# Projections with tokens outermost, one pool for weight buffers, and layer-2 masks on VectorE, in a two-layer decoder trunk

## The chip, the cores and the metric

The kernel runs on one core of one Trainium2 chip. The metric is device time in microseconds (us) of one execution. Before the change the median of three runs is 376.45 us (376.45, 374.06 and 377.89).

## What is computed

Two layers, each on a sequence of 256 tokens of width 1024; batch 1, everything float32.

```python
for l in range(2):
    mod = c @ w_ada[l] + b_ada[l]                 # -> shift, scale, gate, 1024 each
    u   = x * (1 + scale) + shift
    h   = u @ w_in[l]                             # one projection, columns split among groups
    o   = concat[DSA(4 heads), FoX(6 heads), NSA(6 heads)] * silu(h_gate)
    x   = LayerNorm(4 ** 0.25 * x + (1 + gate) * (o @ w_out[l]))
# DSA: causal attention over 64 keys picked per token by an indexer (scores, top-k -> mask)
# FoX: causal attention with a cumulative forget term added to the scores
# NSA: two causal branches and one over compressed keys, mixed by gates
# masked softmax: s = where(mask, s, -inf); e = exp(s - max(s)); e / sum(e)
```

## The kernel before, in words

The 256 tokens are two blocks t0 and t1 of 128. Heads go in pairs; a layer makes 11 calls of `attn_pair`: 2 for DSA, 6 for NSA (3 pairs, 2 branches each) and 3 for FoX.

**Weights.** All of them come from one packed array as a stream of pieces of 128 x 1024 floats (512 KB), in a fixed order. SP issues the loads (L487, in `load_more`); a load waits for a free slot among 6 "raw" buffers. A piece of a projection weight is then split in two: ACT casts it to fp32r, the high part wh (L518, `split_hi`); DVE subtracts wh from raw, which gives the low part wl (L536, `split_lo`). The raw slot is free once wl is written. There are 5 wh and 5 wl buffers, free when the last matmul of the piece is done (`piece_done`). Each product of two such operands is three matmuls on PE (`mm3`, L551 to L553). Pieces of the conditioning weight w_ada aren't split: DVE multiplies and sums each in one instruction (L585, "ada").

**Order.** Each engine runs its instructions in one fixed order. A planner (`Order`) makes it when the program is built: every part of the work is a task with a priority, an engine and a modelled cost, and the task that could go and has the smallest priority number goes next. `PR` (L364) holds the priorities (`nsa1=5.08`: NSA of layer 2, and so on) and the orders of tiles (`tord0`, `tord1`).

**Stages.** Layer 1 takes 64 pieces for its chunks A to D (token-major products: q, k, v, gates) as they arrive. Then come 16 "tiles" T (L551 with 128x256 outputs; 8 hold FoX and NSA operands, 8 the output gate), interleaved with rope (L643 to L646), transposes of it (L657), attention, and the ada pieces of layer 2.

**Attention.** In `attn_pair` PE writes the scores of two heads for t0 (128 columns each) and t1 (256 columns) into PSUM (L724); FoX adds its cumulative term by a matmul (L729), and the mask is added by another: L732 adds the DSA mask, L734 the causal triangle. DVE takes the negated row maximum (L679), ACT the exponential from PSUM with the row sum (L683), DVE the reciprocal of the sums (L669 on), ACT the normalisation (L696); PE transposes (L706), ACT copies to SBUF (L710), PE multiplies with V (L755).

**Output projection.** Eight pieces O.n.q (n: half of the 1024 columns, q: quarter of the contraction). The loop is n outside t: n0 for t0 and t1 (512 columns each), then n1 for t0 and for t1, in two blocks of 256 columns each. After each block `resid` runs on DVE: times gate (L1229), plus scaled x (L1232), row statistics (L1234). When a token block has all of its columns, the mean and variance follow (L1244, L1245), a reciprocal square root on ACT and DVE (L1291 to L1295), and for layer 1 `next_u`: transposes of the normalised rows (L1376), their high part uH and low part uL (L1402) for layer 2. In layer 2 the rows are finished (t0: L1280, L1286; t1: L1301, L1304) and stored.

**Layer 2** begins with chunks in the order D, C, A, B (`proj_tok`): for D the loop is t outside q, so that t0 can begin before t1 is ready; for C, A and B it is q outside t.

Of the kernel before, what the change touches and what calls it, by code (L numbers as in the profile page):

```python
# [362 lines left out]
RW = [6, 5]  # L363
PR = dict(zn='VV', upart=4, ul='VVVV', nrm='AAAA', cord='DCAB', t1q=0, cuts=(0, 512, 1024), oq=(0, 1, 2, 3), tord=(0, 1, 2, 3, 4, 5, 6, 7, 8, 9, 10, 11, 12, 13, 14, 15), gpp=(0, 1), res=-3.5, warm=10, tol=0.1, ada_at=(10, 0.5), adag_at=((0, 0.5), (8, 1)), ow=(512, 256), aff=0.49, tw=512, nact=((0, 0), (1, 0), (0, 1), (1, 1)), pro='', gp0=(0, 1), gp1=(0, 1), acc=5, s=2, pt=1, o=3, ms=3, side=8, topk=3, idx=2, dec=0.5, cmp=1.2, nsa=1.6, dsa=1.7, fox=1.8, gate=4, gate1=6, ada=6, main=10, ev=0, split=4, nahead=2, acc1=1.5, cmp1=3, dec0=0.28, nsa1=5.08, topk1=5.9, nsa0=1.3, dec1=0.5, idx1=0.64, tord1=(2, 4, 6, 7, 0, 1, 8, 9, 5, 3, 14, 10, 12, 13, 11, 15), dsa0=0.12, oq0=(1, 0, 2, 3), cmp0=1.39, fox1=1.95, dsa1=4.17, fox0=1.48, oq1=(1, 3, 2, 0), topk0=3, tord0=(0, 1, 3, 4, 5, 6, 7, 8, 9, 10, 11, 12, 13, 2, 14, 15), idx0=2, nrm1='AAAA', nrm0='AAAA', t1q0=0, t1q1=0)  # L364
# [3 lines left out]
def trunk(ctx: ExitStack, tc: tile.TileContext, xT, x, crow, wst, bcol, lnrow, pe_b, cst, cstb, out,  # L368
# [105 lines left out]
    def load_more():  # L474
        while nload[0] < len(order):
# [10 lines left out]
            t = wp.tile([P, 1024], F32, tag="raw", name=nm("raw"), bufs=RAW)  # L486
# [39 lines left out]
    def split_lo(key, on_pool):  # L526
# [5 lines left out]
        lo = wp.tile([P, 1024], F32R, tag="wl", name=nm("wl"), bufs=WH)  # L532
        if on_pool:
            G.tensor_tensor(lo[:, :n], raw, h[:, :n].bitcast(F32), op=ALU.subtract)
        else:
            V.tensor_tensor(lo[:, :n], raw, h[:, :n].bitcast(F32), op=ALU.subtract)  # L536
# [3 lines left out]
        raw_done()  # L540
# [228 lines left out]
    def layer(l, uH, uL):  # L769
# [211 lines left out]
        def dsa_pair(i, prio):  # L981
# [499 lines left out]
```

## Time and profile before

| | |
|---|---|
| median of three runs | 376.45 us |
| the profiled execution | 374.79 us |
| its span (first to last instruction) | 373.0 us |
| mean granted TensorE clock in it, as a share of full speed | 0.978 |
| instructions | 6834 |
| weights moved on SP's queue | 74.75 MB |

The span is cut here in six stages: 0 to 58.4 us is the chunk projections of layer 1 with their loads; to 146.6 us tiles and attention up to the last DSA scores; to 172.8 us the rest of the attention and the last tiles; to 221.4 us the output projection of layer 1, the hand-over to layer 2 and its chunks D and C; to 363.1 us the rest of layer 2, to its last matmul; then the end. In the table of windows "PEclk" is the clock that TensorE was granted, "DMA share" the mean busy share of 16 DMA engines. In a list of instructions in order of time, square brackets hold the time for which the engine stood idle just before and what ended it.

### The profile page before, as it was taken

Reading aid. Unit: us, or ns where it says so; the run is one execution under the profiler, and the core shown is the slowest. Engines: PE = TensorE matmul, PEld = TensorE weight load, DVE = VectorE, ACT = ScalarE, POOL = GpSimd, SP = SyncE. Lnnn points to the kernel's source line nnn. Section 1 sums busy time; section 2 is a strip of 40 time slices with the busy share of each in tenths; the row PEclk is TensorE's granted clock in tenths of the full one; section 3 lists DMA queues with packets and bytes.
Section 4 is the critical chain, followed back from the end, with each engine's and each line's share of the span. In section 5 each row is a group of like instructions: output and inputs, shape, how many; then the busy total and the mean of one; then the engine's idle time right before and its main releaser. Section 6 shows DMA issues by size and latency. Waiting matters only on the chain.

```text
span 373.0 us, 6834 instructions
## 1 busy us (share of the span) xinstructions
PE 344.9 (92%) x2430; PEld 282.7 (76%) x2430; DVE 314.8 (84%) x771; ACT 251.7 (67%) x656; POOL 2.5 (1%) x10
## 2 busy tenths in 40 slices
PE   6899999699999997879987999999999999999990
PEld 2688769579887785777986888678887887887890
DVE  5798889999989989889979985989988894666876
ACT  3554566769898785595558764667897868997420
POOL 2000000000000000000000000000000000000000
PEclk9899999989999999899999999999999999999996
DMA  6999999456763167979728486543436865123003
GB/s 217 416 406 402 352 368 397 152 160 210 238 205 126 57 183 222 317 241 330 253 71 268 146 293 192 162 123 112 128 104 199 306 198 197 58 59 112 1 2 112
DMA packets 22074, 75.47 MB, mean 202 GB/s; under 512 B 2964, under 2 KB 3096, under 8 KB 21912
## 3 DMA queue, kind: packets, MB, share of 16 engines
q1 hardware_dynamic: 21752, 74.75, 59.5%
q8 instruction: 19, 0.31, 0.3%
q10 hardware_dynamic: 288, 0.29, 0.2%
q14 instruction: 15, 0.12, 0.1%
HBM read 73.98 MB, written 1.05 MB: 201 GB/s over the span
## 4 chain that ended last, share of the span: by engine, by line
PE 70%; DMA 12%; DVE 11%; ACT 4%; issue 2%; SPq 0%; DVEq 0%; ACTq 0%
PE b L551 16%; PE b L553 15%; PE b L552 15%; DMA raw<-in_wst_dram 12%; PE b L724 5%; PE b L755 5%; PE b L706 4%; DVE raw L585 2%; DVE wl L536 2%; ACT wh L518 2%; PE b L657 2%; PE b L734 2%; PE b L908 2%; ACT t2k L1384 1%; PE b L627 1%
## 5 line engine op out<-in xcount | busy, mean ns | idle before, releaser
L518 ACT CAST wh<-raw 128x1024 fp32r<-128x1024 f32 (+2 forms) x81 | 83.2, 1028 | 48.6 <-DMA raw<-in_wst_dram 29.8
L536 DVE TENSOR_TENSOR wl<-raw,wh 128x1024 fp32r<-128x1024 f32 (+2 forms) x81 | 96.0, 1193 | 14.4 <-ACT wh L518 13.4
L551 PE MATMUL b<-uH,wh 128*128 128x256 f32 x256 | 78.0, 305 | 0.0
L552 PE MATMUL b<-uL,wh 128*128 128x256 f32 x256 | 73.0, 285 | 0.0
L553 PE MATMUL b<-uH,wl 128*128 128x256 f32 x256 | 73.0, 285 | 0.0
L585 DVE SCALAR_TENSOR_TENSOR raw<-raw,cbc 128x1024 f32<-128x1024 f32 x48 | 58.2, 1217 | 3.9 <-DMA raw<-in_wst_dram 3.8
L553 PE MATMUL b<-wh,uL 128*128 128x512 f32 (+1 forms) x128 | 50.6, 395 | 2.7 <-DVE uL L1358 1.5
L551 PE MATMUL b<-wh,uH 128*128 128x512 f32 (+1 forms) x128 | 51.0, 399 | 2.0 <-ACT uH L1356 2.0
L551 PEld LDWEIGHTS b<-uH,wh 128*128 128x128 f32 x256 | 49.7, 194 | 2.0 <-issue 1.3
L552 PE MATMUL b<-wl,uH 128*128 128x512 f32 (+1 forms) x128 | 50.2, 392 | 0.3 <-DVE wl L536 0.3
L552 PEld LDWEIGHTS b<-uL,wh 128*128 128x128 f32 x256 | 49.8, 194 | 0.0
L553 PEld LDWEIGHTS b<-uH,wl 128*128 128x128 f32 x256 | 49.5, 193 | 0.1
L683 ACT ACTIVATE p<-b,nmx 128x128 f32<-128x128 f32 x88 | 36.3, 427 | 1.5 <-DVE nmx L679 1.4
L696 ACT ACTIVATE p<-p,rinv 128x128 f32<-128x128 f32 (+1 forms) x88 | 34.5, 454 | 1.5 <-DVE rinv L672 1.4
L553 PEld LDWEIGHTS b<-wh,uL 128*128 128x128 f32 x128 | 24.4, 191 | 9.8 <-DVE uL L1358 3.5
L551 PE MATMUL b<-wh,mH 128*128 128x256 f32 (+1 forms) x96 | 31.3, 326 | 0.0
L553 PE MATMUL b<-wh,mL 128*128 128x256 f32 (+1 forms) x96 | 30.7, 320 | 0.0
L552 PE MATMUL b<-wl,mH 128*128 128x256 f32 (+1 forms) x96 | 30.6, 319 | 0.0
L551 PEld LDWEIGHTS b<-wh,uH 128*128 128x128 f32 x128 | 24.5, 191 | 7.6 <-ACT uH L1356 2.9
L552 PEld LDWEIGHTS b<-wl,uH 128*128 128x128 f32 x128 | 24.3, 190 | 5.1 <-DVE wl L536 1.1
L710 ACT COPY pT<-b 128x384 f32<-128x384 f32 x44 | 21.2, 484 | 8.5 <-PE b L706 8.3
L679 DVE TENSOR_REDUCE nmx<-b 128x1 f32<-128x128 f32 x88 | 25.4, 347 | 0.3 <-PE b L734 0.2
(173 smaller groups left out, 557.2 us busy)
## 6 DMA issues: line engine op xcount, KB each, us to landing
raw<-in_wst_dram SPq DMA_DIRECT2D x120, 512.0 KB, 4.8
raw<-in_wst_dram SPq DMA_DIRECT2D x7, 480.0 KB, 6.6
lnr<-in_lnrow_dram SPq DMA_DIRECT2D x4, 512.0 KB, 4.8
raw<-in_wst_dram SPq DMA_DIRECT2D x4, 448.0 KB, 4.4
xT_sb<-in_xT_dram SPq DMA_DIRECT2D x4, 256.0 KB, 6.7
x_sb<-in_x_dram SPq DMA_DIRECT2D x1, 1024.0 KB, 7.9
out_dram<-x_sb SPq DMA_DIRECT2D x3, 256.0 KB, 2.2
cf<-in_cst_dram SPq DMA_DIRECT2D x1, 384.0 KB
```

What stands on the lines that cost most here:

```text
L518: A.copy(h[:, :n], loaded[key])
L536: V.tensor_tensor(lo[:, :n], raw, h[:, :n].bitcast(F32), op=ALU.subtract)
L551: T.matmul(o, ah, bh, start=start, stop=False)
L552: T.matmul(o, ah, bl, start=False, stop=False)
L553: T.matmul(o, al, bh, start=False, stop=stop)
L585: V.scalar_tensor_tensor(w, w, 1.0, cbc, op0=ALU.mult, op1=ALU.mult, accum_out=mods[l][:, j, h:h + 1])
L679: V.tensor_reduce(nmx[:, t, a:a + 1], so[:, P * t:P * t + P * (t + 1)], axis=AX.X, op=ALU.max, negate=True)
L683: A.activation(p_sb[:, P * t:P * t + P * (t + 1)], so[:, P * t:P * t + P * (t + 1)], AF.Exp, bias=nmx[:, t, a:a + 1], accum_out=st[:, t, a ...
L696: A.mul(blk, blk, r[:, t, a:a + 1])
L710: A.copy(pT, pt.rearrange("p a b -> p (a b)"))
L724: T.matmul(sp[a][:, P * t:P * t + nk], qT[r, t * P:(t + 1) * P], kT[r, :nk], start=True, stop=False, skip_group_check=True)
L755: T.matmul(O[64 * a:64 * a + 64, P * kt:], vs(a, kt), outs[a][0][:, 256 * kt:256 + 128 * kt], start=(first and kt == 0), stop=(last and kt ...
```

## The change

- `tout=(1, 1)`: the output projections of both layers loop t outside n. t0: n0 and n1, 512 columns each; t1: n0 with 512, n1 with two blocks of 256. All eight O pieces stay until t1 has used them.
- `tch=2`: chunks D and C of layer 2 are one loop with t outermost (t0: D, C; t1: D, C). Their eight pieces stay until t1.
- Raw, wh and wl take their buffers from one pool of 20 (before 6 + 5 + 5 = 16). Up to 11 raw pieces may be out; one counts as gone only when its piece has been used up (`piece_done`), not when it has been split. `SCRATCH` is a smaller scratch for dynamic DMAs, and the "u" buffers join "sg": both make room.
- `vmask=('', 'dnf')`: in layer 2 no mask matmuls. DVE adds the mask to the scores, negates, writes the result p to SBUF and takes the row minimum in the same instruction (L680 of the changed kernel); the exponential reads p from SBUF with scale -1, and the PSUM bank is free after DVE.
- Priorities: `dsa0` 0.12 to 1.48, `cmp0` 1.39 to 1.12, two tiles swapped in `tord1`, tile 5 moved behind tile 2 in `tord0`.

```diff
-RW = [6, 5]
+SCRATCH = 1024
+RW = [11, 8]
-    t = wp.tile([P, 1024], F32, tag="raw", name=nm("raw"), bufs=RAW)
+    t = wp.tile([P, 1024], F32, tag="w", name=nm("raw"), bufs=RAW + WH + 1)
 ...                                    # wh and wl likewise; then in split_lo and piece_done:
         od.set("w", key)
-        raw_done()
 ...
         od.release("wh")
+        raw_done()
 ...
+        if mask is not None:           # head_exp
+            p_sb = buf("p", 384)
+            for t in range(2):
+                blk = slice(P * t, P * t + P * (t + 1))
+                V.tensor_tensor_reduce(p_sb[:, blk], so[:, blk], mask[t], -1.0, 3.0e38, op0=ALU.add, op1=ALU.min,
+                                       accum_out=nmx[:, t, a:a + 1])
+            unbank("s")
+            for t in range(2):
+                A.activation(p_sb[:, blk], p_sb[:, blk], AF.Exp, bias=nmx[:, t, a:a + 1], scale=-1.0,
+                             accum_out=st[:, t, a:a + 1])
 ...
+                if onv:                # attn_pair: no mask matmul
+                    continue
 ...
-            for t, q in units:         # proj_tok
+            units = [(t, c, q) for t in range(2) for c in cs for q in range(4)] if t_outer else ...
 ...
-        for n in range(2):             # output projection
-            w = PR["ow"][n]
-            for t in range(2):
+        blocks = [(n, t) for t in range(2) for n in range(2)] if PR["tout"][l] else [...]
+        for n, t in blocks:
+            w = PR["ow"][n] if not PR["tout"][l] else PR["ow"][n if t else 0]
```

What this moves is seen in the order of instructions on an engine. On PE in layer 1, between the transposes of FoX's and NSA's rope results ("roped", the first after DSA's own), before:

```order
L657 MATMUL b_822<-cf,roped_803 128x128 x2
L657 MATMUL b_840<-cf,roped_828 128x128 x3
L657 MATMUL b_847<-cf,chunk_763 128x128 x3
L551 MATMUL b_701<-uH_104,wh_834 128x256
L552 MATMUL b_701<-uL_105,wh_834 128x256
```

and now:

```order
L655 MATMUL b_813<-cf,roped_786 128x128 x2
L549 MATMUL b_711<-uH_104,wh_776 128x256
...
L655 MATMUL b_852<-cf,roped_821 128x128 x2
L549 MATMUL b_711<-uH_104,wh_776 128x256
...
L655 MATMUL b_877<-cf,roped_844 128x128 x3
L655 MATMUL b_884<-cf,chunk_773 128x128 x3
```

The eight transposes stood together; now the 24 matmuls of one tile (b_711) are spread between them, 12 in each gap.

On PE in layer 2, the scores of one NSA pair (two heads, b_3131 and b_3132), before:

```order
L724 MATMUL b_3131<-q_582_2434,q_588_2440 128x128
L724 MATMUL b_3132<-q_582_2434,q_588_2440 128x128
L734 LDWEIGHTS cb
L734 MATMUL b_3131<-cb 128x128
L734 LDWEIGHTS cb
L734 MATMUL b_3132<-cb 128x128
L724 MATMUL b_3131<-q_582_2434,q_588_2440 128x256
L724 MATMUL b_3132<-q_582_2434,q_588_2440 128x256
```

and now such a pair on DVE, after a split:

```order
L534 TENSOR_TENSOR wl_3259<-raw_3161,wh_3235 128x1024
L680 ISA p_3282,nmx_3250<-b_3244,cf 128x128
L680 ISA nmx_3250 128x1
L680 ISA p_3282,nmx_3250<-b_3244,cf 128x256
L680 ISA nmx_3250 128x1
```

The mask matmuls with their weight loads are gone from PE; DVE has, in place of one maximum for each block, one masked maximum and a second small instruction that writes the row result.

On DVE in the output projection of layer 1 ("t2k" and "x_sb" are `resid`, "mod" and "raw" are ada), before:

```order
L1229 TENSOR_TENSOR t2k_2216<-b_2125,row_1662 128x512
L1232 SCALAR_TENSOR_TENSOR x_sb<-x_sb,t2k_2216 128x512
L1234 BN_STATS bn_2124<-x_sb 128x6 x2
L536 TENSOR_TENSOR wl_2229<-raw_2130,wh_2221 128x1024
L536 TENSOR_TENSOR wl_2241<-raw_2149,wh_2233 128x1024
L536 TENSOR_TENSOR wl_2254<-raw_2163,wh_2245 128x1024
L1229 TENSOR_TENSOR t2k_2266<-b_2204,row_1662 128x512
```

and now:

```order
L1251 TENSOR_TENSOR t2k_2210<-b_2086,row_1749 128x512
L534 TENSOR_TENSOR wl_2212<-raw_2143,wh_2188 128x1024
L1254 SCALAR_TENSOR_TENSOR x_sb<-x_sb,t2k_2210 128x512
L1256 BN_STATS bn_2085<-x_sb 128x6 x2
L534 TENSOR_TENSOR wl_2229<-raw_2159,wh_2200 128x1024
L583 SCALAR_TENSOR_TENSOR raw_1849,mod_91<-raw_1849,cbc 128x1024
L583 SCALAR_TENSOR_TENSOR raw_1894,mod_91<-raw_1894,cbc 128x1024
L1251 TENSOR_TENSOR t2k_2253<-b_2199,row_1749 128x512
L583 SCALAR_TENSOR_TENSOR raw_1901,mod_91<-raw_1901,cbc 128x1024
```

All eight O pieces are split by the second `resid` block, which is now t0's last; and three ada pieces that came before the projection now stand beside it.

On DVE at the end of layer 2 (x_sb with lnr at L1286, L1308 of the changed kernel, finishes rows of t0), before:

```order
L1286 TENSOR_TENSOR x_sb<-x_sb,lnr_4291 128x512 x3
L1229 TENSOR_TENSOR t2k_4549<-b_4512,row_3908 128x256
L1232 SCALAR_TENSOR_TENSOR x_sb<-x_sb,t2k_4549 128x256
L1234 BN_STATS bn_4290<-x_sb 128x6
L1244 BN_AGGR mv_4553<-bn_4290 128x2
```

and now:

```order
L1308 TENSOR_TENSOR x_sb<-x_sb,lnr_4215 128x512
L1254 SCALAR_TENSOR_TENSOR x_sb<-x_sb,t2k_4395 128x512
L1256 BN_STATS bn_4214<-x_sb 128x6 x2
L1251 TENSOR_TENSOR t2k_4421<-b_4385,row_3984 128x256
L1254 SCALAR_TENSOR_TENSOR x_sb<-x_sb,t2k_4421 128x256
L1256 BN_STATS bn_4214<-x_sb 128x6
L1251 TENSOR_TENSOR t2k_4449<-b_4420,row_3984 128x256
```

The finishing of t0 stood ahead of the last block of t1; now three blocks of t1 follow it.

## Rows read from the trace of the kernel before

**Rows 1.** Busy time of each engine, its share of the span and its instructions, from the page.

```profile
PE 344.9 (92%) x2430; PEld 282.7 (76%) x2430; DVE 314.8 (84%) x771; ACT 251.7 (67%) x656; POOL 2.5 (1%) x10
```

**Rows 2.** The six stages: start and end, length in us, then busy us and count of PE, PEld, DVE, ACT and POOL, the granted clock, the DMA share, GB/s.

```profile
0.00:58.40 58.40, 51.61 (x211) 38.68 (x212) 46.29 (x76) 28.71 (x43) 2.48 (x10) 0.97 0.96 361
58.40:146.60 88.20, 85.32 (x733) 69.96 (x731) 83.07 (x256) 69.67 (x221) 0.00 (x0) 0.98 0.59 189
146.60:172.80 26.20, 21.04 (x144) 17.09 (x143) 23.27 (x49) 21.00 (x55) 0.00 (x0) 0.93 0.85 283
172.80:221.40 48.60, 44.86 (x257) 38.80 (x256) 43.91 (x78) 29.93 (x61) 0.00 (x0) 1.00 0.64 211
221.40:363.10 141.70, 141.70 (x1089) 117.96 (x1089) 111.93 (x303) 101.86 (x277) 0.00 (x0) 1.00 0.42 134
363.10:373.00 9.90, 0.41 (x4) 0.21 (x2) 6.34 (x14) 0.50 (x2) 0.00 (x0) 0.70 0.28 106
```

**Rows 3.** The same columns for four short windows: two at the start, one after the longest wait of PE in layer 1, and one in the middle of layer 2.

```profile
6.00:9.00 3.00, 2.60 (x7) 0.60 (x4) 2.04 (x6) 1.04 (x1) 0.00 (x0) 1.00 0.87 237
9.00:12.00 3.00, 1.18 (x4) 0.71 (x5) 1.43 (x2) 2.04 (x3) 0.00 (x0) 1.00 1.02 413
74.00:77.00 3.00, 3.00 (x15) 3.00 (x16) 2.97 (x7) 1.46 (x7) 0.00 (x0) 0.52 0.79 240
240.00:280.00 40.00, 40.00 (x318) 32.94 (x315) 37.11 (x111) 30.93 (x90) 0.00 (x0) 1.00 0.43 129
```

**Rows 4.** PE's instructions in order of time (start us, us, engine, line): those that ended its longer idle times in layer 1.

```profile
73.97 0.87 PE L657 MATMUL b<-cf,roped 128*128 128x128 f32 x3 [2.22 <-DVE roped L646]
...
148.50 0.45 PE L706 MATMUL b<-cf,p 128*128 128x128 f32 x1 [1.73 <-ACT p L696]
...
204.13 0.55 PE L657 MATMUL b<-cf,roped 128*128 128x128 f32 x3 [2.02 <-DVE roped L646]
```

**Rows 5.** The same of ACT at 158 to 160 us; then, from PE's, what came of it.

```profile
158.30 1.04 ACT L518 CAST wh<-raw 128x1024 fp32r<-128x1024 f32 x1 [2.14 <-DMA raw<-in_wst_dram]
159.25 0.85 ACT L710 COPY pT<-b 128x384 f32<-128x384 f32 x2
...
159.78 1.03 PE L755 MATMUL b<-pT,vall 128*64 128x256 f32 x6 [2.44 <-ACT pT L710]
```

**Rows 6.** PE in order of time around the mask matmuls of one NSA, one FoX and one DSA pair of layer 2.

```profile
251.14 0.28 PE L734 MATMUL b<-cb 128*128 128x128 bf16 x2
251.35 0.70 PE L724 MATMUL b<-q,q 64*128 64x256 f32 x4
251.99 0.28 PE L734 MATMUL b<-cb 128*128 128x128 bf16 x2
252.11 0.39 PE L657 MATMUL b<-cf,roped 128*128 128x128 f32 x2
...
304.91 0.22 PE L734 MATMUL b<-cb 128*128 128x128 bf16 x1
304.97 0.22 PE L729 MATMUL b<-cum,cb 96*128 96x128 bf16 x1
...
324.64 0.28 PE L732 MATMUL b<-dmask,cb 128*128 128x128 bf16 x2
324.86 0.70 PE L724 MATMUL b<-q,q 64*128 64x256 f32 x4
325.49 0.39 PE L732 MATMUL b<-dmask,cb 128*128 128x256 bf16 x2
325.72 0.49 PE L706 MATMUL b<-cf,p 128*128 128x128 f32 x3
```

**Rows 7.** Groups of instructions, shapes apart: line, engine, operation, out<-in, count | busy us, mean ns of one | idle before.

```profile
L679 DVE TENSOR_REDUCE nmx<-b 128x1 f32<-128x256 f32 x44 | 18.2, 413 | 0.0
L679 DVE TENSOR_REDUCE nmx<-b 128x1 f32<-128x128 f32 x44 | 12.4, 281 | 0.3 <-PE b L734 0.2
L585 DVE DVE_READ_ACCUMULATOR raw<-raw,cbc 128x1 f32 x48 | 3.9, 82 | 0.0
L585 DVE SCALAR_TENSOR_TENSOR raw<-raw,cbc 128x1024 f32<-128x1024 f32 x48 | 58.2, 1217 | 3.9 <-DMA raw<-in_wst_dram 3.8
L536 DVE TENSOR_TENSOR wl<-raw,wh 128x1024 fp32r<-128x1024 f32 x68 | 82.4, 1220 | 13.0 <-ACT wh L518 12.0
L1131 DVE SCALAR_TENSOR_TENSOR sg<-sg,b 128x256 f32<-128x256 f32 x16 | 6.7, 419 | 7.1 <-ACT sg L1129 7.1
L683 ACT ACTIVATE p<-b,nmx 128x128 f32<-128x128 f32 x44 | 16.5, 374 | 1.5 <-DVE nmx L679 1.4
L696 ACT ACTIVATE p<-p,rinv 128x128 f32<-128x128 f32 x44 | 15.6, 403 | 1.5 <-DVE rinv L672 1.4
```

**Rows 8.** The last matmuls of the program and DVE after it, in order of time.

```profile
363.12 0.28 PE L552 MATMUL b<-wl,mH 128*128 128x256 f32 x1
363.24 0.28 PE L553 MATMUL b<-wh,mL 128*128 128x256 f32 x1
...
362.94 2.00 DVE L1286 TENSOR_TENSOR x_sb<-x_sb,lnr 128x512 f32<-128x512 f32 x3
364.86 0.42 DVE L1229 TENSOR_TENSOR t2k<-b,row 128x256 f32<-128x256 f32 x1
```

**Rows 9.** The loads of weight pieces: line, queue, operation, count, KB each, median us from issue to landing.

```profile
raw<-in_wst_dram SPq DMA_DIRECT2D x120, 512.0 KB, 4.8
```

More of the change, by code (lines that the diff above doesn't have):

```diff
@@ L531, in split_lo @@
         h = ready[key]
[L532 to L536, printed above, removed]
+        lo = wp.tile([P, 1024], F32R, tag="w", name=nm("wl"), bufs=RAW + WH + 1)
+        (G if on_pool else V).tensor_tensor(lo[:, :n], raw, h[:, :n].bitcast(F32), op=ALU.subtract)
         ready[key] = (h[:, :n], lo[:, :n])
@@ L713, in head_pt, with attn_pair @@
         od.set(*ev)
-    def attn_pair(l, qT, kT, vs, obox, first, last, mask=None, cum=None, gate=None, prio=1):
-        yield until(("raw", ("cb",)))
+    def attn_pair(l, kind, qT, kT, vs, obox, first, last, mask=None, cum=None, gate=None, prio=1):
+        yield until(("raw", ("cb",)), ("raw", ("masks",)))
         yield bank("s", 2)
-        yield ("P", 2 * fmm(128, 256) + (0.35 if mask is not None else 0.24) + (0.35 if cum is not None else 0))
+        onv = kind in PR["vmask"][l]
+        yield ("P", 2 * fmm(128, 256) + (0 if onv else 0.35 if mask is not None else 0.24) + (0.35 if cum is not None else 0))
         sp = [ps(384) for _ in range(2)]
@@ L734, in attn_pair @@
                     T.matmul(so[:, nk - P:], ident_b, diag_b, start=False, stop=True, skip_group_check=True)
+        vm = None if not onv else (causal[:, P:], causal) if mask is None else (mask[:, 0:P], mask[:, P:])
         nmx = small([P, 2, 2], "nmx", 6)
@@ L1145, in out_gate, with proj_tok @@
             od.set("m", l, i)
[L1148 to L1154 removed]
+        def proj_tok(cs, t_outer=False):
+            accs = {}
+            units = [(t, c, q) for t in range(2) for c in cs for q in range(4)] if t_outer else \
+                    [(t, c, q) for c in cs for q in range(4) for t in range(2)]
+            for t, c, q in units:
+                n = len(CHUNKS[c])
+                if (c, t) not in accs:
+                    yield bank("acc")
+                    accs[c, t] = ps(n)
                 yield until(("u", l, t, q // 2), ("w", (c, l, q)))
@@ L1213, in layer @@
         else:
-            for c in PR["cord"]:
-                yield from proj_tok(c, t_outer=(c == PR["cord"][0]))
+            n = PR["tch"]
+            yield from proj_tok(PR["cord"][:n], True)
+            for c in PR["cord"][n:]:
+                yield from proj_tok(c)
         evac = [evac_kv] * 2 + [evac_fox] * 6
@@ new lines, in layer @@
+        oq = pr("oq", l)
+        blocks = [(n, t) for t in range(2) for n in range(2)] if PR["tout"][l] else [(n, t) for n in range(2) for t in range(2)]
+        for n, t in blocks:
+            w = PR["ow"][n] if not PR["tout"][l] else PR["ow"][n if t else 0]
+            for i in range(512 // w):
+                o = w * i
+                yield bank("acc")
+                acc = ps(w)
+                for q in oq:
+                    key = ("O", l, n, q)
+                    yield until(("m", l, 2 * q), ("m", l, 2 * q + 1), ("w", key))
+                    yield ("P", rmm(w, 6))
+                    h, lo = piece(key, 512)
+                    mH, mL = mix
+                    for k in (2 * q, 2 * q + 1):
+                        ts = slice(t * P, (t + 1) * P)
+                        cs = slice(o, o + w)
+                        mm3(acc, mH[:, k, ts], mL[:, k, ts], h[:, k % 2, cs], lo[:, k % 2, cs],
+                            k == 2 * oq[0], k == 2 * oq[-1] + 1)
+                    if t == 1 and i == 512 // w - 1:
+                        piece_done(key)
+                if n == 1 and t == 0 and i == 0:
+                    A.preload_act_table_set("natural_log_exp_and_others")
+                od.spawn(resid(t, 512 * n + o, w, acc), PR["res"])
```

75 lines of the change are left out of this document (23 added, 52 removed).

## The prediction, as it was made before the changed kernel ran

> **What bounds the kernel now.** I read four views in this order. The busy times of the engines come first: TensorE (PE) is busy for 92% of the span, VectorE (DVE) for 84%, ScalarE (ACT) for 67% [rows 1]. An average over stages hides where the other 8% of PE lies, so the table of stages is second [rows 2]; what is to be seen is PE's busy time beside each length. From 221.4 to 363.1 us PE is busy for 141.70 of 141.70 us, at full clock: that stage is as long as its matmuls. PE's idle time is in layer 1: 6.8 us up to 58.4, 2.9 up to 146.6, 5.2 up to 172.8 and 3.7 up to 221.4; at the end of the program come 9.9 us without PE. Two stages have a reduced clock besides: 0.98 over 88.2 us and 0.93 over 26.2 us are 1.8 us each of full-speed work lost. Third, the short windows [rows 3] show where: right behind PE's wait at 73.97 the granted clock is 0.52, the lower of its two levels (1.2 GHz of 2.4), for 3 us. So a wait there is paid for twice. Fourth, PE's waits in order of time [rows 4, 5]: before rope transposes, before attention's transposes, before the product with V. No wait for weights stands among them. But DVE is busy for 83.07 of 88.2 us in the second stage and 37.11 of 40 in the middle of layer 2 [rows 2, 3]; it is never far behind PE as the bound, and this change gives it more to do.
>
> **Parts of the sum.** It is made against the profiled execution, 374.79 us (span 373.0 and 1.8 around it). The median is 376.45, that is 1.66 above; I add that at the end.
>
> 1. *Start (pool of 20).* Before, six loads fill the raw buffers, and the seventh waits for a split. The bytes show it: 237 GB/s from 6 to 9 us, 413 in the next 3 us [rows 3], and 361 over the stage, which is bound by its loads (DMA share 0.96) [rows 2]. With 11 slots, the loads go on. Three microseconds at 361 instead of 237 save 3 x 124/361 = 1.0 us; by 413, 1.3; nothing if the later splits decide. I take -1.0 (0 to -1.3).
>
> 2. *Up to the last DSA scores.* On PE the eight rope transposes stood in a row, the third group waiting 2.22 us for DVE's rope [rows 4], and half speed came after [rows 3]: 3 us at 0.52 lose 1.4 us. Now 12 matmuls of a tile stand in each gap, at 0.12 us each (the step between the rows of two such matmuls, 363.12 and 363.24 [rows 8]) 1.4 us each: 2.9 us of work for a wait of 2.2. Everything idle here is 2.9, with the clock 4.3: the most that can go. Against it: DVE is idle for 5.1 us of 88.2 only, and by the order the split of tile 2 (1.22 us [rows 7]) and a normaliser now stand on it ahead of the last DSA maximum, which costs 1.5 if nothing covers it. I take the middle of 4.3 and 0, -2.2 (+1.5 to -4.3).
>
> 3. *To the end of the tiles, up to 172.8.* One tile moves from here to the stage before; that is no gain in itself. PE waits 2.44 us for a copy of pT on ACT, which stood behind a cast whose load came late (ACT idle 2.14 us, then 1.04 for the cast) [rows 5]. With more slots, that load is issued some 20 us ahead of its use by the order of SP, so the cast is ready when ACT comes to it. The wait of 1.73 for p [rows 4] stays, since it is a chain of attention. What is late next is the first O pieces: their splits stand behind the last folds of attention on DVE. I take -2.2 (+1 to all that is idle, -5.2).
>
> 4. *Output projection and hand-over, up to 221.4.* A block of 24 matmuls with 512 columns takes 24 x 0.23 = 5.5 us (twice the step of 256 columns). With t outside, t0 is whole after two blocks and not after three: 5.5 us earlier for PE. But by the order, between the first `resid` and the end of t0 DVE then has 2 splits, 3 ada pieces and two `resid` blocks to do, and four splits directly ahead of them: 6 x 1.22 + 3 x (1.22 + 0.08) [rows 7] + 2 x some 2.1 (three 512-column instructions at 2.00/3 [rows 8]) = 15.4 us, against 11.0 us of PE. t0 is whole when DVE is done, about 1 us earlier than the 16.5 us of three blocks before. Behind that the hand-over has two blocks of t1 on PE to cover it, not one, so the wait of 2.02 us [rows 4] could go; new ones come where t1's pieces wait for DVE. I take -0.5 (+3 to -3).
>
> `tch=2` is within that: t0's matmuls for two chunks (2 x 24 at 448 or 512 columns, some 10 us) stand before the first that needs t1. Its price is eight pieces that stay until t1; with wh and wl in a pool of 20, they fit. The wait that it adds, of SP on PE's last use of a piece, has all later loads queued behind it. A load takes 4.8 us to land [rows 9], a cast 1.04 and a split 1.22: a load that is issued 7.1 us ahead of its turn costs nothing.
>
> 5. *Masks of layer 2.* On PE, two mask matmuls of 128 columns take 251.35 - 251.14 = 0.21 us and the second two 0.12 [rows 6]: 0.33 for each of 6 NSA calls. FoX: from the mask matmul at 304.91 to the next instruction at 304.97 it is 0.06 us; four of them are 0.24, times 3 calls. DSA: 0.22 + 0.23 = 0.45, times 2. Sum 2.0 + 0.7 + 0.9 = 3.6 us, in a stage where PE is never idle: the gain is full if nothing else becomes late.
> DVE pays. Before, a head costs maxima of 281 + 413 ns; the masked maximum isn't in the trace. If it runs as fast as a maximum and adds the second small instruction, as ada does (82 ns [rows 7]), it is 44 x 0.082 = 3.6 us more in layer 2 (22 heads, two blocks each). If it takes two passes, it adds an instruction over 384 columns per head, at 419 ns for 256 (L1131) and half of it above 1220/1024 x 128, some 0.70 us, in all 15.5 us. Nothing suggests a gain on DVE; a lower bound is 0. I take 3.6, since L585 too does two operations and a sum in one pass: 1217 ns for 1024 columns, while the plain subtraction L536 takes 1220 [rows 7].
> The Trainium skill says in "Vector Engine (DVE) Microarchitecture Reference", section "Points that are easy to get wrong", that the accumulating scalar-tensor-tensor form halves its throughput with two SBUF sources that aren't bf16. L585 is that case in this trace and isn't halved against L536; the scores come from PSUM, so only one source here is SBUF. By that rule masks would cost DVE some 10 us, an estimate of mine (384 columns x 1.19 ns more for each of 22 heads), which lies within the bounds above and ends in rival B.
> DVE is idle for 29.8 us of stage 5, but for only 2.9 from 240 to 280 us [rows 2, 3], where four of the NSA calls are: 16 x 0.082 = 1.3 us more there leave it at 38.4 of 38.7 us. Some of the gain will be lost there, so I take -3.0 (+0.5 to -4.3).
> ACT's exponential takes its input from SBUF: L683 from PSUM takes 374 ns, L696 from SBUF 403 [rows 7]; 44 x 0.03 = 1.3 us more, hidden by ACT's 39.8 idle us.
>
> 6. *End.* PE's last matmul starts at 363.24 and is done by 363.5; DVE takes its result at 364.86, since three instructions of t0's finishing (2.00 us) stand ahead [rows 8]. Now t0 is finished long before: -1.3 (-0.9 to -1.9).
>
> Sum: -1.0 - 2.2 - 2.2 - 0.5 - 3.0 - 1.3 = -10.2. 374.8 - 10.2 = 364.6; with 1.66, **366.2 us**.
>
> **Rivals.**
> *A. DVE holds layer 1.* Tiles, splits and ropes take the same DVE time as before, so the reordering moves waits and takes none away: parts 2 to 4 give 0. For it: 83.07 of 88.2 us busy [rows 2]; against it: in the third stage DVE has 2.9 idle us of 26.2, and the wait at 159.78 came from a load. -5.3, so 371.2 us.
> *B. The masked maximum takes two passes.* From 240 to 280 us eight heads cost 8 x 0.70 = 5.6 us more on a DVE with 2.9 idle: 2.7 us late, and the 1.3 of masks on PE there isn't gained. Masks give +0.4 instead of -3.0: 369.6 us. For it: two operations and an accumulation on one instruction; against it: L585.
> *C. Slower: a cast and its split fall behind each other.* The t-outer loops need 8 O pieces and 8 of D and C before any is freed; loads after that are issued only when t1 uses pieces up. Where a load is issued less than 7.1 us ahead of its split, ACT's 1.04 comes in front of DVE's 1.22 with neither covering the other: 16 pieces x 1.1 = 17.6 us on the path. 374.8 + 17.6 - 10.2 + 0.5 (part 4 not gained) + 1.66 = 384.4 us. For it: the first piece of D is loaded when the last O split is done, by the order 13 DVE instructions (6 to 7 us) before its own split, right at the point; against it: later pieces have more slack, and DVE's ada pieces lie between.
> *D. Layer 1's waits go altogether,* with the half clock behind them: part 2 gives -4.3, part 3 -6.0: 360.3 us. For it: 7 us of idle time and clock in the third stage; against it: the chain of attention there remains.
>
> **How the numbers follow.** My forecast 0.55, A 0.21, B 0.10, C 0.07, D 0.07. A measurement of this kernel tells a difference of about 1% from none: that is below 372.7 or above 380.2 us. Faster: 0.54 of the forecast, 0.16 of A (which lies only 1.5 us below the limit), 0.08 of B, 0.07 of D, together 0.85. The same: 0.01 + 0.05 + 0.02 = 0.08. Slower: C, 0.07. The range leaves out C above and half of D below, with little of A: 359 to 373 us.
>
> **What would show it.** Part 1: no dip in GB/s from 6 to 9 us. Part 2: no wait over 1 us at the third group of rope transposes, and a clock near 1 behind it. Part 3: PE's wait for pT gone, ACT not waiting for a load there. Part 4: PE idle for some 3 us from the first output projection to the first matmul of chunk A; above 7 speaks for C. Part 5: PE still without idle time in layer 2 and 3 us less of it; the masked maximum at about 281 and 413 ns (281 + 286 or more in place of 281 is B). Part 6: DVE takes the last block within 0.3 us of PE's end. I am wrong if PE in layer 2 waits for DVE, or if PE's idle time in layer 1 stays at 18 us.

## The result, and the profile after

The changed kernel takes 359.64 us (median of four runs, 359.52 to 360.43), the kernel before 377.02 beside it (374.06 to 377.89): a ratio of 0.956, 95% interval 0.950 to 0.961. Forecast were 366.2 us and a range of 359 to 373. The time is at the range's lower edge: 17.4 us went, where 10.2 were expected. The profiled execution takes 359.52 us, 15.3 less than that of before; the sum is read against it.

The stages of the changed kernel, in the columns of [rows 2], cut at the same work: first tile, fifth group of output-projection matmuls, first matmul of chunk A, last matmul. Then the first two short windows of [rows 3]. Cut at the same work, the stages of before are 58.38, 114.43, 48.64 and 141.79 us long; that is a few hundredths off [rows 2], and the differences here and below are to these.

```profile
0.00:57.03 57.03, 49.95 (x210) 38.59 (x211) 46.55 (x78) 28.78 (x43) 2.48 (x10) 0.97 0.98 377
57.03:163.07 106.04, 104.20 (x875) 84.70 (x874) 101.93 (x300) 89.55 (x275) 0.00 (x0) 1.00 0.67 232
163.07:211.57 48.50, 44.91 (x235) 37.43 (x234) 46.73 (x83) 32.31 (x62) 0.00 (x0) 1.00 0.62 211
211.57:349.28 137.71, 137.26 (x1022) 114.01 (x1021) 112.59 (x344) 98.66 (x275) 0.00 (x0) 1.00 0.42 135
6.00:9.00 3.00, 2.35 (x8) 0.68 (x6) 2.13 (x6) 1.04 (x1) 0.00 (x0) 1.00 0.89 239
9.00:12.00 3.00, 1.31 (x3) 0.70 (x4) 1.64 (x2) 1.95 (x3) 0.00 (x0) 0.82 1.02 417
```

The second row answers to the second and third of [rows 2] together: 114.4 us before, 106.04 now. PE's idle time in it fell from 8.1 to 1.8 us, its busy time from 106.4 to 104.2 at the same number of matmuls, with the granted clock at 1.00 and no longer at 0.98 and 0.93. DVE's busy time fell from 106.3 to 101.9. With the ends of the stages, the saving is: start 1.35, tiles and attention 8.4, hand-over 0.1, layer 2 4.1, end 1.35 (what lies behind the start of the last matmul).

PE's idle times from the first tile on, in order of time, as in [rows 4, 5]:

```profile
108.33 0.86 PE L773 MATMUL b<-pT,vall 128*64 128x256 f32 x6 [0.48 <-ACT pT L724]
145.23 0.44 PE L720 MATMUL b<-cf,p 128*128 128x128 f32 x2 [0.36 <-ACT p L710]
147.96 0.86 PE L773 MATMUL b<-pT,vall 128*64 128x256 f32 x6 [0.44 <-ACT pT L724]
162.74 0.50 PE L551 MATMUL b<-wh,mL 128*128 128x512 f32 x1 [0.29 <-DVE mL L1161]
164.21 0.50 PE L550 MATMUL b<-wl,mH 128*128 128x512 f32 x1 [0.75 <-DVE wl L534]
172.38 0.50 PE L550 MATMUL b<-wl,mH 128*128 128x512 f32 x1 [0.84 <-DVE wl L534]
181.20 0.63 PE L1390 MATMUL b<-cf,x_sb 128*128 128x128 f32 x4 [0.51 <-issue]
190.56 0.47 PE L551 MATMUL b<-wh,uL 128*128 128x448 f32 x1 [1.10 <-DVE uL L1416]
209.55 0.55 PE L655 MATMUL b<-cf,roped 128*128 128x128 f32 x3 [0.38 <-DVE roped L644]
255.22 0.86 PE L773 MATMUL b<-pT,vall 128*64 128x256 f32 x6 [0.37 <-ACT pT L724]
```

No wait for the rope transposes of layer 1 is left, and no wait over 1.1 us. New are PE's waits for weights (wl, 0.75 and 0.84 us) in the output projection.

The masked maximum with the causal mask, and the second instruction of all 44 masked maxima (groups, shapes apart, as [rows 7]):

```profile
L680 DVE CUSTOM_DVE_ANT_0 p<-b,cf 128x256 f32<-128x256 f32 x18 | 7.5, 419 | 0.0
L680 DVE CUSTOM_DVE_ANT_0 p<-b,cf 128x128 f32<-128x128 f32 x18 | 5.1, 283 | 0.6 <-PE b L744 0.6
L680 DVE DVE_READ_ACCUMULATOR2_ANT nmx<- 128x1 f32 x44 | 3.6, 82 | 0.0
```

283 and 419 ns stand against 281 and 413 of the plain maximum, and 82 ns for the second. The rule of the Trainium skill that the prediction weighed ("Vector Engine (DVE) Microarchitecture Reference", "Points that are easy to get wrong") speaks of two SBUF sources; with one of them in PSUM, this trace shows no halving.

The end, as [rows 8]: PE's last matmul and DVE after it.

```profile
349.28 0.28 PE L551 MATMUL b<-wh,mL 128*128 128x256 f32 x1
...
348.42 0.43 DVE L1256 BATCH_NORM_STATS2 bn<-x_sb 128x6 f32<-128x256 f32 x1
349.60 0.42 DVE L1251 TENSOR_TENSOR t2k<-b,row 128x256 f32<-128x256 f32 x1 [0.75 <-PE b L551]
```

DVE now waits for PE, 0.75 us, and takes the last block 0.04 us after the matmul's end.

### The profile page after: what moved, and what is told of

The parts are those of the page before. It is cut to its first block, busy times and chain, and to the rows that moved or that the text cites. A ratio compares the mean times of both kernels' runs of the same rounds, so it can differ in the third digit from the quotient of the medians.

```text
span 357.7 us, 6693 instructions
## 1 busy us (share of the span) xinstructions
PE 336.6 (94%) x2338; PEld 274.8 (77%) x2338; DVE 312.4 (87%) x811; ACT 249.8 (70%) x656; POOL 2.5 (1%) x10
## 4 chain that ended last, share of the span: by engine, by line
PE 41%; DVE 7%; ACT 3%; issue 2%; DVEq 0%; ACTq 0%
PE b L549 10%; PE b L551 10%; PE b L550 10%; DVE wl L534 3%; PE b L773 2%; PE b L720 2%; PE b L739 2%; ACT p L686 1%; PE b L1030 1%; PE b L655 1%; PE b L926 1%; ACT p L710 1%; PE b L625 1%; DVE bn L1256 0%; DVE x_sb L1254 0%
## 5 line engine op out<-in xcount | busy, mean ns | idle before, releaser
L534 DVE TENSOR_TENSOR wl<-raw,wh 128x1024 fp32r<-128x1024 f32 (+2 forms) x81 | 96.2, 1194 | 10.2 <-ACT wh L519 4.9
L549 PE MATMUL b<-uH,wh 128*128 128x256 f32 x256 | 76.5, 299 | 0.0
L550 PE MATMUL b<-uL,wh 128*128 128x256 f32 x256 | 72.2, 282 | 0.0
L549 PEld LDWEIGHTS b<-uH,wh 128*128 128x128 f32 x256 | 48.7, 190 | 3.4 <-issue 2.3
L551 PEld LDWEIGHTS b<-uH,wl 128*128 128x128 f32 x256 | 48.7, 190 | 0.4 <-DVE wl L534 0.2
L550 PEld LDWEIGHTS b<-uL,wh 128*128 128x128 f32 x256 | 48.8, 191 | 0.0
L550 PE MATMUL b<-wl,mH 128*128 128x512 f32 (+1 forms) x80 | 28.1, 351 | 1.6 <-DVE wl L534 1.6
L549 PE MATMUL b<-wh,mH 128*128 128x512 f32 (+1 forms) x80 | 28.5, 356 | 0.1
L551 PE MATMUL b<-wh,mL 128*128 128x512 f32 (+1 forms) x80 | 27.9, 349 | 0.3 <-DVE mL L1161 0.3
L773 PE MATMUL b<-pT,vall 128*64 128x256 f32 (+1 forms) x176 | 21.7, 339 | 1.4 <-ACT pT L724 1.3
L720 PE MATMUL b<-cf,p 128*128 128x128 f32 x132 | 22.4, 281 | 0.5 <-ACT p L710 0.4
```

The source lines that it names most:

```text
L534: (G if on_pool else V).tensor_tensor(lo[:, :n], raw, h[:, :n].bitcast(F32), op=ALU.subtract)
L549: T.matmul(o, ah, bh, start=start, stop=False)
L550: T.matmul(o, ah, bl, start=False, stop=False)
L551: T.matmul(o, al, bh, start=False, stop=stop)
L720: T.transpose(pt[:, i, :], p_sb[:, P * i:P * i + P], ident)
L773: T.matmul(O[64 * a:64 * a + 64, P * kt:], vs(a, kt), outs[a][0][:, 256 * kt:256 + 128 * kt], start=(first and kt == 0), stop=(last and kt ...
```

## The experiments

The question was which edit brought 8.4 us between the first tile and the projection where 4.4 were forecast, and whether DVE or PE's order decides. The kernel before took 376.2, 377.05 and 376.9 us beside the three groups of runs (e1 to e4, e5 to e8, e9 to e12). Ratios are to it. The changed kernel was not run again beside them, so a difference to it of a microsecond or two (e7's) is the least certain. "Planned anew" means that the planner made new orders for the edited program; "in the plan of the changed kernel", that the orders stayed.

**Pool and priorities by themselves (e1, e2, e3).** All three have the old loops and masks on PE, and are planned anew.

```diff
 # e1: pool only, e3: pool and the changed priorities (both from the changed kernel)
-PR = dict(tout=(1, 1), tch=2, vmask=('', 'dnf'), ...
+PR = dict(tout=(0, 0), tch=1, vmask=('', ''), ...
 ...                                    # e1 also has dsa0, cmp0, tord0 and tord1 as before
 # e2: the kernel before with the changed priorities and tile orders
-dsa0=0.12, cmp0=1.39, tord0=(0, 1, 3, 4, 5, ...), tord1=(..., 10, 12, ...)
+dsa0=1.48, cmp0=1.12, tord0=[0, 1, 3, 4, 6, ...], tord1=[..., 12, 10, ...]
```

> The kernel before with the one pool of 20 buffers alone (old loops, old priorities, masks on PE). From the first tile of layer 1 to the fifth group of output-projection matmuls the changed kernel is 8.4 us shorter, where 4.4 were forecast. If the pool brings that (loads come earlier, so no cast waits with other work of ACT queued behind it): about 367 to 369 us, with PE's wait for pT and the half clock gone. If the new order of tiles and priorities brings it: the start alone is gained, 375 to 376 us.

> The kernel before with the changed priorities and tile orders alone, three separate pools as before. If the order brings the 8.4 us (matmuls of a tile between the rope transposes, dsa later): 368 to 371 us and a clock near 1 around the rope transposes. If the pool brings them: 376 to 378 us. If only both together do: this and the pool alone each stay above 373.

> The kernel before with pool and priorities, but old loops and masks on PE. If the loops and masks have no part in layer 1 up to the output projection: 377.0 - 1.35 - 8.4 = 367.3 us, and the rest (4.1 of layer 2, 1.3 at the end, 0.1 at the hand-over) is what the loops and masks add. Above 370 us the t-outer loop of layer 1 would have a hand in the earlier stages.

Measured: e1 375.7 us (ratio 1.000, 0.997 to 1.003), e2 378.7 (1.006, 1.002 to 1.009), e3 376.2 (0.999, 0.996 to 1.002). None is faster than before. For e3 some 367 us were written, 9 too few; e1's time is the one written for a gain at the start alone, but its stages say otherwise: first e1's (tiles and attention, hand-over, layer 2), then e2's (tiles and attention), then e3's (as e1's).

```profile
57.15:167.02 109.87, 104.36 (x876) 84.29 (x874) 103.75 (x298) 90.56 (x274) 0.00 (x0) 1.00 0.63 221
167.02:218.73 51.71, 45.20 (x257) 38.85 (x257) 48.63 (x86) 32.28 (x63) 0.00 (x0) 1.00 0.62 206
218.73:364.06 145.33, 143.99 (x1091) 118.52 (x1089) 109.52 (x301) 98.10 (x275) 0.00 (x0) 1.00 0.38 124
```

```profile
60.20:173.46 113.26, 105.14 (x875) 84.58 (x874) 106.36 (x303) 89.96 (x273) 0.00 (x0) 1.00 0.64 214
```

```profile
57.11:163.15 106.04, 104.19 (x876) 84.74 (x874) 101.91 (x298) 89.52 (x275) 0.00 (x0) 1.00 0.65 232
163.15:218.35 55.20, 47.66 (x258) 41.38 (x256) 48.08 (x83) 32.80 (x63) 0.00 (x0) 0.91 0.54 186
218.35:364.59 146.24, 143.96 (x1091) 118.52 (x1089) 110.47 (x302) 98.08 (x274) 0.00 (x0) 1.00 0.38 123
```

With both, every engine has the order of the changed kernel up to the projection, and the stage takes the same 106.04 us: loops and masks have no part in the 8.4 us. That the time is above 370 us does not mean, as was written for e3, that the loop has a hand in the earlier stages. With the pool alone the stage is 4.6 us shorter than before, with the priorities alone 1.2.

How far such a difference can be trusted is seen in e6 (below), whose layer 1 has the order of before on every engine. Its tiles and attention, and its hand-over, in its profiled execution:

```profile
57.62:175.01 117.39, 108.89 (x875) 89.44 (x874) 106.60 (x303) 90.50 (x275) 0.00 (x0) 0.94 0.63 207
175.01:225.53 50.52, 46.42 (x257) 40.16 (x256) 44.44 (x79) 29.43 (x60) 0.00 (x0) 0.97 0.63 209
```

In one order the first took 114.4 us in one execution, with a granted clock of 0.97, and 117.4 in another, with 0.94. So the 1.2 us of e2 can't be told from nothing, the 4.6 of e1 only just, and the 8.4 may be some 3 us more. The order of the changed kernel repeats better: 106.03 to 106.14 us in its eight profiles (after, e3, e4, e5, e7, e8, e10, e11). One part of the split is plain: e2 still has the wait of 2.22 us for a rope transpose (the last section shows it), e1 has none over 0.4 us for them in layer 1. The matmuls between the transposes came with the pool, not with the priorities.

But e3 gives all of it back: the hand-over takes 55.2 us (48.6 before) and layer 2 146.2 (141.8). In the hand-over PE's longest waits, and the clock in windows around them, are:

```profile
188.16 1.94 PE L1390 MATMUL b<-cf,x_sb 128*128 128x128 f32 x8 [4.13 <-issue]
192.72 0.74 PE L549 MATMUL b<-wh,uH 128*128 128x448 f32 x1 [2.61 <-ACT uH L1412]
```

```profile
189.00:192.00 3.00, 1.10 (x6) 0.70 (x4) 2.93 (x6) 2.68 (x7) 0.00 (x0) 0.50 1.03 418
192.00:195.00 3.00, 2.29 (x6) 1.90 (x7) 2.87 (x7) 2.69 (x7) 0.00 (x0) 0.50 0.54 216
195.00:198.00 3.00, 3.00 (x11) 2.68 (x10) 1.04 (x2) 1.75 (x5) 0.00 (x0) 0.53 0.55 175
```

DVE is busy for 48.1 us in e3's hand-over against 43.9 before. Three ada pieces start there (before, one), two of them (180.90 and 182.84 us) directly ahead of t0's mean and variance (183.97); of splits it is 19 (before, 16). So in the hand-over part of the early gain was work of DVE's put off, which the old loops can't carry. That does not explain layer 2: e1's is 3.5 us longer than before too, and so is that of e4 below (144.12 us) by 2.3, which has the new loops. Pool and masks on PE, planned anew, make a longer layer 2 with either loops.

**The loops (e8, e11, e7).** Each is the changed kernel with one loop as before.

```diff
-PR = dict(tout=(1, 1), tch=2, ...
+PR = dict(tout=(0, 1), tch=2, ...      # e8: layer 1's projection
+PR = dict(tout=(1, 1), tch=1, ...      # e11: chunk C of layer 2
+PR = dict(tout=(1, 0), tch=2, ...      # e7: layer 2's projection
```

> The changed kernel with the old loop in layer 1's output projection alone. With pool and priorities but all loops old, the hand-over took 55.2 us against 48.5. If the loop of layer 1's projection decides that (DVE has three ada pieces more ahead of the mean and variance, and the hand-over then covers them with two blocks of PE instead of one): 365 to 367 us, PE waiting 3 to 4 us for the transposes of the normalised rows. If it is the t-outer loop of chunks D and C: 360 to 362 us here.

> The changed kernel with chunk C of layer 2 by the old loop (q outside t), D alone t-outer. C's first matmuls then need t1's uL half as many matmuls later: t0's share of C, 24 matmuls of 0.23 us = 5.5 us, no longer stands ahead of them. If the hand-over needs that cover: 2 to 5 us more, 362 to 364.5 us, as longer waits for uL of t1. If t-outer in the projection is enough: 359.6 to 360.5 us.

> The changed kernel with the old loop in the last output projection alone (n outside t). If that loop does nothing but take t0's finishing off the end: 359.6 + 1.3 = 360.9 us, all of it behind the last matmul. If holding eight pieces until t1 also served or hurt the stage before, the last matmul moves by more than 0.5 us.

Measured: e8 368.4 us (0.979, 0.973 to 0.985), 8.8 above the changed kernel and above what was written; e11 364.7 (0.969, 0.966 to 0.972), 5.0 above; e7 361.3 (0.960, 0.954 to 0.966), 1.7 above. The hand-over of e8, then of e11, against 48.50:

```profile
163.26:219.69 56.43, 47.48 (x259) 41.18 (x258) 48.91 (x86) 33.51 (x65) 0.00 (x0) 0.91 0.52 175
```

```profile
163.21:216.68 53.47, 47.08 (x233) 38.38 (x232) 49.80 (x83) 32.97 (x63) 0.00 (x0) 0.97 0.58 192
```

All that these two lose is in the hand-over, give or take 0.9 us: e8's PE waits 4.13 us before the transposes of the normalised rows, as e3's does, and 2.61 for uH. In e11 longer waits for uL were expected, but that for uL is 1.10 us as in the changed kernel; new are waits for normalised rows (1.08 and 0.94 us). Both loops are needed, and either alone doesn't do: the two losses, 8.8 and 5.0, sum to more than the 6.6 us that the hand-over of e3 lost. In e7's profile layer 2 up to the last matmul takes 0.4 us more (138.08), and what lies behind it 9.8 us where the changed kernel has 8.4: part 6 measured by itself.

**The masks (e4, e5, e6).**

```diff
 # e4: the changed kernel, masks on PE, planned anew
-vmask=('', 'dnf')
+vmask=('', '')
 # e5: masks on PE in the plan of the changed kernel
-                V.tensor_tensor_reduce(p_sb[:, blk], so[:, blk], mask[t], -1.0, 3.0e38, ...
+                V.tensor_reduce(nmx[:, t, a:a + 1], so[:, blk], axis=AX.X, op=ALU.max, negate=True)
 ...
-                A.activation(p_sb[:, blk], p_sb[:, blk], AF.Exp, ..., scale=-1.0, ...
+                A.activation(p_sb[:, blk], so[:, blk], AF.Exp, ...
 ...
-                if onv:
-                    continue
 # e6: the kernel before with vmask=('', 'dnf') alone, planned anew
```

> The changed kernel with layer 2's masks added by PE again. By the count of matmuls (0.33, 0.24 and 0.45 us for each NSA, FoX and DSA call: 3.6 us, in a stage where PE never waits) 363.2 us. If DVE were the bound there, and the longer work on it cost what PE gains (rival B): 359 to 360.5 us.

> The changed kernel with the plan unchanged (each engine's other instructions in the same order as with the masks on DVE), but the mask matmuls of layer 2 back on PE, a plain maximum on DVE and the exponential from PSUM. The run with masks on PE and a plan of its own was 6.6 us longer, where the count of matmuls gives 3.6. If only the matmuls count: 363.2 us, and the other 3 us were the plan's. If masks on PE really cost more than their spacing in the trace of before (waits for a free score bank, now held until the exponential): 365 to 366.5 us.

> The kernel before with the masks of layer 2 on DVE and nothing else. By the count of matmuls 376.4 - 3.6 = 372.8 us, with PE still without idle time in layer 2. If DVE is the bound there without the larger pool (37.11 of 40 us busy from 240 to 280 us, 1.3 us more by the second small instruction): 375 to 377 us, and PE waits for wl in the middle of layer 2.

Measured: e4 366.2 us (0.972, 0.967 to 0.978), 6.6 above the changed kernel and above both cases that were written; e5 363.0 (0.964, 0.958 to 0.971), 3.4 above; e6 376.1 (1.000, 0.996 to 1.004), nothing won. Layer 2 of e4 and of e5, then of e6 with two of PE's waits in it:

```profile
211.85:355.97 144.12, 143.36 (x1067) 117.13 (x1065) 112.26 (x300) 98.00 (x275) 0.00 (x0) 1.00 0.39 129
211.70:352.68 140.98, 140.98 (x1066) 116.68 (x1065) 112.56 (x300) 97.68 (x275) 0.00 (x0) 1.00 0.41 132
```

```profile
225.53:367.48 141.95, 140.44 (x1046) 116.10 (x1045) 112.10 (x347) 102.78 (x277) 0.00 (x0) 1.00 0.41 132
```

```profile
333.52 1.55 PE L775 MATMUL b<-pT,vall 128*64 128x256 f32 x8 [0.74 <-ACT pT L726]
...
349.82 0.50 PE L551 MATMUL b<-wh,mH 128*128 128x512 f32 x1 [0.46 <-ACT mH L1161]
```

In one plan the masks are worth 140.98 - 137.71 = 3.3 us, near the 3.6 counted. On the kernel before, planned anew, they are worth nothing: the profiled layer 2 takes 141.95 us (141.79 before). PE's waits for wl, which were written for this case, are not there; PE, with less to do, waits in the last attention pairs for their chain through ACT and DVE, as the two rows show. Its idle time went from 0 to 1.5 us, and its busy time fell by 1.4 only, not by 3.6; how much of that is the waits and how much the new order was not taken apart. The count of matmuls is a saving only where something covers that chain; the other 3.2 us of e4 are its plan's.

**DVE as the bound (e9, e12, e10).**

```diff
 # e9: layer 2's ada pieces earlier in the planner's list, planned anew
-ada_at=[10, 0.5]
+ada_at=[8, 0.5]
 # e12: every sixth split of layer 1's tiles and O pieces on GpSimd, planned anew
-gp0=(0, 1)
+gp0=(1, 6)
 # e10: the masked maximum in two passes, in the plan of the changed kernel
-                V.tensor_tensor_reduce(p_sb[:, blk], so[:, blk], mask[t], -1.0, 3.0e38, ...
+                V.tensor_tensor(p_sb[:, blk], so[:, blk], mask[t], op=ALU.add)
+                V.tensor_reduce(nmx[:, t, a:a + 1], p_sb[:, blk], axis=AX.X, op=ALU.max, negate=True)
 ...                                    # and the exponential without scale=-1.0
```

> The changed kernel with the ada pieces of layer 2 two places earlier in the planner's list, so that three of them (3.9 us of DVE) stand ahead of the last attention of layer 1 again, as before, and not in the output projection. If the 8.4 us between the first tile and the projection came from taking that DVE work out of a stage that DVE binds: that stage grows from 106.0 to some 109.5 us, the hand-over loses its waits for wl and uL (up to 2.5 us), and the time is 360.6 to 363 us. If it came from PE's order and the earlier loads alone: the stage stays within 1 us of 106, and the time is 357.5 to 359.7 us, since the hand-over gets shorter.

> The changed kernel with every sixth split of layer 1's tiles and O pieces on GpSimd, which is idle there: 4 splits, 4.9 us less for DVE. If DVE still binds the stages from the first tile to chunk A: 356.5 to 358.5 us (PE's remaining waits there are 1.8 and 3.6 us). If PE does by now: 359 to 360 us. If a split on GpSimd is so slow that PE waits for it, or slows DVE beside it: 360.5 us or more.

> The changed kernel in the same plan, with the masked maximum of layer 2 in two passes on DVE (addition to SBUF, then a maximum), as rival B supposed: some 0.53 us more for each of 22 heads, 11.7 us of DVE in layer 2, where DVE is idle for 25 us of 137.7. If DVE were close to the bound there, as rival B says, at least the 2.7 us that it forecasts: 362 to 366 us. If its slack is enough and only the chains of the last pairs get longer: 360 to 361 us.

Measured: e9 368.5 us (0.979, 0.976 to 0.983), e12 369.4 (0.981, 0.977 to 0.985), e10 368.7 (0.979, 0.976 to 0.983). e9 and e10 are slower than any case that was written of them; e12 lies in its third case (360.5 us or more). e9's stages:

```profile
56.75:168.55 111.80, 106.66 (x867) 86.66 (x866) 105.58 (x301) 90.38 (x273) 0.00 (x0) 0.97 0.64 225
168.55:220.50 51.95, 46.94 (x246) 39.08 (x244) 44.68 (x82) 32.17 (x65) 0.00 (x0) 0.97 0.56 188
```

The edit did less than it was meant to: one ada piece more starts in the stage (20, 19 in the changed kernel), with two splits more (20 and 18). DVE has 3.7 us more to do there and the stage takes 5.8 us more. That agrees with a stage that DVE holds. So do the stage's lengths over the orders on record, each beside DVE's busy time in it: 106.04 us at 101.9, 109.87 at 103.8 (e1), 111.80 at 105.6 (e9), 113.3 and 114.4 at 106.4 (e2, before), 117.4 at 106.6 (e6). It isn't a proof: a longer stage also takes in more of DVE's pieces, the planner put other work of PE elsewhere too, and the hand-over, with less for DVE, got 3.5 us longer instead of shorter, with 2.82 us of waiting for mH at 173.82. What share of the 8.4 us is DVE's work and what the order of tiles stays open.

e12 was to relieve DVE, and did not. A split takes GpSimd 2.4 to 3.2 us where DVE takes 1.22, and two DVE instructions that started during one lasted far longer than elsewhere:

```profile
L534 POOL TENSOR_TENSOR wl<-raw,wh 128x1024 fp32r<-128x1024 f32 x4 | 10.6, 2643 | 149.2 <-ACT wh L519 71.1 <-DVE rinv L667 40.0 <-DVE rinv L670 38.1
```

```profile
77.35 2.35 DVE L969 SCALAR_TENSOR_TENSOR fx<-fx,fx 128x12 f32<-128x12 f32 x1
160.50 3.41 DVE L583 SCALAR_TENSOR_TENSOR raw<-raw,cbc 128x1024 f32<-128x1024 f32 x1
```

In the changed kernel the first takes 0.17 us and the second 1.22; here GpSimd's splits ran from 76.50 to 79.66 and from 160.19 to 162.83 us. Maxima beside a third split, at 117.81, kept their time. So DVE is busy for 313.9 us in all, 312.4 in the changed kernel, although four splits (4.9 us) left it. Both stages got longer (109.9 and 54.4 us), with waits of 2.42 and 1.92 us for mH in the projection. This run says nothing, then, on whether a freer DVE would help; how much of its loss is the slower DVE, the late splits or the plan was not taken apart.

e10 prices rival B. Its layer 2:

```profile
211.97:358.52 146.55, 141.34 (x1022) 115.66 (x1021) 126.74 (x344) 100.65 (x275) 0.00 (x0) 0.99 0.38 127
```

14.2 us more of DVE cost 8.8 us of time, although DVE was idle for 25 us of the stage. PE's idle time rose from 0.45 to 5.2 us, most of it waits for pT and p; its busy time rose by 4.1, in part at a lower clock (0.55 from 260 to 263 us). Idle time of DVE there doesn't absorb work that stands in the chain score, maximum, exponential. Rival B, at 369.6 us against the forecast's 366.2, had 3.4 us for it, less than half of the price.

## Why the prediction came out as it did

The direction and the order of size held, and the mechanisms of parts 5 and 6; part 1 gained elsewhere than named, of parts 2 and 3 the cause is open in part, and part 4 missed what the loops do. The sum of -10.2 was too small, by 5.1 in the profiled execution, and 4.0 of these are in parts 2 and 3. That the time lies within the range, by 0.6 us, is in part luck: the range was drawn around a sum that gave the early stages half of what they gained.

- *Part 1*, -1.0: 1.35 measured, but not by the step that was named. From 6 to 9 us the stream still moves 239 GB/s. It gained later, in windows where the loads had waited for slots: from 36 to 54 us they waited 8.7 us in all for DVE to write wl or finish an ada piece, and now for neither. Before, then after:

```profile
39.00:42.00 3.00, 2.43 (x12) 1.82 (x11) 2.94 (x5) 1.44 (x3) 0.00 (x0) 1.00 1.00 296
48.00:51.00 3.00, 2.70 (x12) 1.92 (x11) 2.97 (x6) 0.90 (x1) 0.00 (x0) 1.00 0.91 300
```

```profile
39.00:42.00 3.00, 2.34 (x12) 1.74 (x11) 2.89 (x5) 1.43 (x3) 0.00 (x0) 1.00 1.02 399
48.00:51.00 3.00, 3.00 (x15) 2.52 (x14) 2.88 (x6) 2.83 (x5) 0.00 (x0) 1.00 1.03 405
```

- *Parts 2 and 3*, -4.4: 8.4 measured; this is the term that was mis-sized. That matmuls of a tile cover the rope wait held. Two steps failed. "The wait of 1.73 for p [...] stays, since it is a chain of attention": now the longest for p is 0.36 us. And DVE's load was taken as given, with 1.5 us added, where two ada pieces and a split left the stage (19 and 18 start in it, 21 and 19 before): by instruction order three ada pieces moved behind the first `resid`, but the third started behind the cut already. Rival D (-10.3) was nearer than the forecast: of 8.1 us of idle time 1.8 are left, and of the lower clock nothing. Rival A (nothing) fell, though its premise, that DVE holds the stage, agrees with e9. How 8.4 divides between DVE's lighter load, PE's new order and the earlier loads is not shown.
- *Part 4*, -0.5: -0.1 measured, and its working held: t0's statistics are complete 15.2 us after the fifth matmul group (178.23 - 163.07), where 15.4 was worked out for DVE; before, it was 15.8 (188.61 - 172.81). What the prediction didn't see is that this near zero is a difference of two large numbers: with the old loops, the same pool and priorities cost 6.6 us here (e3), and that one loop 8.8 (e8). Forecasting each edit against the kernel before, the prediction gave the loops almost nothing; without either of them, the hand-over gives back much of what the others bring.
- *Part 5*, -3.0: 4.1 measured for the stage, 3.3 of it the masks in an equal plan (e5); the same edit on the kernel before gained nothing (e6), so the count needed the changed plan. The 82 ns and the equal speed of the masked maximum were right. The 0.6 us taken off for a crowded DVE was needless: PE's idle time in layer 2 is 0.45 us. The remaining 0.8 is not taken apart.
- *Part 6*, -1.3: 1.35 measured, by the mechanism named (e7).
- *Rival C* did not occur: with t outermost, waits for wl are 0.75 and 0.84 us, not 17.6.
- The median moved by 17.4 us, the profiled executions by 15.3: the difference of 2.1 is that the profiled execution of before lies 2.2 us below its median, that of after 0.1. By e6, executions of the order of before differ in layer 1, so the profile of before was a quick one there.

## What to carry to other kernels

Where engines run in fixed orders, edits are not a sum: pool and priorities (e3) and masks (e6), each planned anew, gained nothing on the kernel before, while masks or one loop taken away from the changed kernel cost 1.7 to 8.8 us (e4, e5, e7, e8, e11). So ask of each gain which later stage receives the work that was moved, and price the edits together there. An engine with idle time in a stage still binds it if its work stands in a chain that others wait for (e10).

## What was not expected of the hardware

From the end of PE's wait of 4.13 us in e3 on, and through the one of 2.61, the granted clock was at the lower level for some 9 us (0.50 to 0.53 from 189 to 198 us), so that the same matmuls of the hand-over kept PE busy 47.7 instead of 44.9 us. In the changed kernel, where no wait after the first tile is over 1.1 us, it stays at 1.00.

One wait of some 2 us does not decide it. Up to the rope transposes, e2 has PE's order of before and the same wait of 2.22 us, but not the clock of 0.52 behind it [rows 3]:

```profile
75.78 0.52 PE L657 MATMUL b<-cf,roped 128*128 128x128 f32 x3 [2.22 <-DVE roped L646]
```

```profile
76.00:79.00 3.00, 3.00 (x23) 2.23 (x21) 2.93 (x8) 1.35 (x7) 0.00 (x0) 1.00 0.68 217
```

With the wait of 2.02 us in the hand-over [rows 4] it is the other way round: before, it was followed by 1.00 (204 to 207 us); in e6, with the same order and the same wait, ended at 206.65, by 0.70 and 0.73 (206 to 212 us). So the clock behind one and the same wait differs between executions. In the eight profiles with the changed kernel's order of tiles and attention the wait is gone, and the clock of that stage is 1.00 in each.
